# New order of work in the paired up-projection of layer 1, with its DRAM weight sums moved out of the attention

## The chip, the cores and the metric

One NeuronCore of one Trainium2 chip runs the whole network in one launch. The metric is device microseconds of one execution; a time given for a kernel is the median of its runs. In the profile PE is the matmul engine (PEld its weight loads), DVE the vector engine, ACT the scalar engine, POOL GpSimd; SP only issues DMAs, and POOL issues some too.

## The reference

A two-layer trunk on 512 tokens of width 1024 in fp32: layer 0 mixes tokens by gated linear attention (GLA), layer 1 by sparse attention with shared keys and values (NSA); each is followed by an output projection and a convolutional feed-forward. The change lies in the feed-forward of layer 1 and in what is prepared for it:

```python
def conv_ffn(x, w_up, conv_w, conv_b, w_down):
    S = x.shape[1]
    u = x @ w_up                                   # 1024 -> 2 x 2816
    u_pad = jnp.pad(u, ((0, 0), (CONV_WIDTH - 1, 0), (0, 0)))
    hc = conv_b
    for j in range(CONV_WIDTH):                    # 3 taps along the tokens
        hc = hc + conv_w[j] * u_pad[:, j:j + S]
    a, b = split_cols(hc, (FFN_DIM, FFN_DIM))
    return (jax.nn.silu(a) * b) @ w_down

h = h + conv_ffn(rmsnorm(h, norm_ffn[i]), w_up[i], conv_w[i], conv_b[i], w_down[i])
```

## The kernel before

**Precision.** Every fp32 operand of a matmul is split into a high and a low part: `split_to` lets ACT copy the high part into an fp32r tile and DVE subtract it from the source to give the low part. A product is then three matmuls (high by high, low by high, high by low). The weight tiles pass through three rings: `wraw` (four raw tiles of 128 x 1024, filled by DMAs that SP issues), and `wh` and `wl` (four split tiles each). A ring's next user waits until the last reader of the tile it takes over has finished.

**Layer 1's feed-forward.** The 2816 hidden columns are 22 blocks of 128, j = 0 to 21, each with two halves (a and b of the reference). A plain half is 24 matmuls of 128x512 into an `acc` bank of PSUM. `conv` applies the taps to a bank: one ACT instruction and two DVE instructions that write the tile `hc`. `gate` forms silu(a) * b and splits it.

From j = 6 to j = 19 the blocks go in seven pairs (`pairs`; `FAST` lists the odd members). The even block of a pair is two plain halves. The odd one is a Strassen-like scheme on 2x2 blocks: seven products of 12 matmuls of 128x256 (`product`, numbered 1 to 7; line 1131) instead of eight. Between them come the products 5, 7 and 6 of the down projection of an earlier pair (`mms`, line 1487): 5 into the banks `sc`, 7 into `po`, 6 into `pt`, six matmuls of 128x512 each. I call these the first, second and third down sum. Banks A and B of `acc` alternate, so that a bank is written again two uses later, once DVE's convolution has read it.

In a pair the names are: `w0`, `w1` the weights of the two plain halves; `w` in turn those of products 1 and 5, of 6 and 7, of 2 and 3; `wd` that of product 4; `wf` those of the first two down sums; `ops[p][6]` that of the third. `old` carries the odd block's second half into the next pair, where `second` finishes it.

**Who sets the order.** PE's matmuls here are chained by `pe`, ACT's and DVE's instructions by `Ordered` (`act.on = dve.on = True`), so each engine runs the pairs in the order in which the code is written, and an engine waits at the head of its queue. SP issues the loads in program order too, four tiles ahead (`load`).

**The sums in DRAM.** The scheme needs sums of quarters of the weight blocks. POOL prepares them in DRAM: `sums` issues four DMAs a block (a copy of 512 KB and three accumulating ones), and `pace` ties each to an instruction of the running part, so that POOL issues it then. `jobs` says which block belongs to which part: D are the 11 blocks of the down projection, U[j] the seven blocks of the up projection. Part `mix1` is the attention of layer 1, in which POOL also multiplies the probabilities P by their gates (`P<-P,ssm`).

Of the kernel before, what the change touches and what calls it, by code (L numbers as in the profile page):

```python
# [23 lines left out]
NJ = FFN // 128  # L24
# [186 lines left out]
class Trunk:  # L211
    def __init__(self, nc, tc, ctx, I, out, W):
# [21 lines left out]
        self.jobs = {"mix0": three(*D[:3]), "ffn0": each(U[7], D[3], U[9], D[4], U[11], D[5]), "mix1": three(U[13], D[6], U[15]),  # L234
                     "ffn1": each(D[7], U[17], D[8], U[19], D[9], D[10])}
# [60 lines left out]
    def early_exp(self):  # L296
        self.tc.keep_in_program_order(self.nc.scalar.activation(self.t(self.small, [128, 64], "ex", bufs=1)[:, 0:1], self.ones[:, 0:1], AF.Exp))
# [315 lines left out]
    def gla_layer(self):  # L613
        nc, I, tc = self.nc, self.I, self.tc
        with ExitStack() as outer:
            pool = outer.enter_context(tc.tile_pool(name="gla", bufs=1))
            mo = [tuple(self.t(pool, [128, S], f"mo{m}{c}", FR) for c in "hl") for m in range(2)]
# [422 lines left out]
    def up(self, l, pool, rows, us, fill, gate, pe, space=None, seven=None):  # L1040
# [44 lines left out]
        def pairs(js):  # L1085
# [6 lines left out]
            items = [(wp[up[2 * js[0]]],)]  # L1092
            for j in js:
                p, b = j // 2 - 1, self.upb(l, j + 1)
                items += [(wp[up[2 * j + 1]],), (q(qs, p, 0, 2),), (q(qd, b, 2), q(qs, b, 0)), (q(qs, b, 2), q(qs, b, 1)), (q(qs, p, 2),),
                          (q(qd, b, 3), q(qs, b, 3)), (q(qd, b, 0),), (wp[up[2 * j + 4]],)]
# [18 lines left out]
            def prep(dst=None):  # L1115
                load()
                w = dst or [self.t(self.wsp, [128, 1024], t, FR) for t in ("wh", "wl")]
                self.split_to(*w, raws.pop(0))
                return w

            def plain(half, dst, w):
                for k in range(KC):
                    o = slice(128 * k, 128 * k + 128)
                    for n, (a, b) in enumerate(((0, 0), (1, 0), (0, 1))):
                        pe(nc.tensor.matmul(dst, w[a][:, o], self.x[k][b], start=k + n == 0, stop=k == KC - 1 and n == 2))  # L1125
# [7 lines left out]
            def step(half, u, dst, *parts):  # L1133
                self.conv(l, cj[0], half, u, dst, parts)
                if "act" in parts:
                    self.pace("ffn1", self.conv_ins)

            def second(old, part):
                j, B, v, hc = old
                cj[0] = j  # L1140
                if part == 0:
                    dve.scalar_tensor_tensor(out=B[:, O], in0=v[:, E], scalar=-1.0, in1=v[:, O], op0=ALU.mult, op1=ALU.subtract)
                    dve.tensor_tensor(out=B[:, E], in0=B[:, E], in1=v[:, E], op=ALU.subtract)
                    step(1, B, hc[1], "act")
                elif part == 1:
                    step(1, B, hc[1], "dve")
                else:
                    gate(j, *hc, False)

            for _ in range(3):  # L1150
                load()
            cj, old = [0], None
            w0 = prep()
            act.on = dve.on = True
            for j in js:
                p, b = j // 2 - 1, self.upb(l, j + 1)
                hc = [self.t(pool, [128, S], "hc0", bufs=3), self.t(pool, [128, S], "hc1")]
# [11 lines left out]
                if j == js[0]:  # L1169
                    forms(2)  # L1170
                v2, = V
                v = v2.rearrange("p a t -> p (a t)")
                cj[0] = j
                step(0, A, hc[0], "act", "dve")
                ops[p] = {5: [t[:, :512] for t in wf], 7: [t[:, 512:] for t in wf]}
                mms(p, (5, 7))
                w = prep()
                step(1, B, hc[1], "act", "dve")
                act.activation(hc[0], hc[0], AF.Silu)
                A, B = (self.ps("acc") for _ in range(2))  # L1180
                product(1, A[:, E], w, 0, True)
                product(5, A[:, O], w, 512)
                w = prep()
                gate(j, *hc, False)
                act.copy(v, A)
                ops[p][6] = prep([self.t(self.tmp, [128, S], "sq", FR, bufs=2) for _ in range(2)])
                product(6, B[:, O], w, 0, True)
                product(7, B[:, E], w, 512)
                w = prep()
                wd = prep(W4[j // 2 % 2])  # L1190
                product(2, A[:, E], w, 0)
                product(3, A[:, O], w, 512)
                w0 = prep()
                dve.tensor_tensor(out=v2, in0=v2, in1=bass.AP(tensor=B.tensor, offset=B.offset + 256, ap=[B.ap[0], [-256, 2], [1, 256]]), op=ALU.subtract)
                mms(p, (6,))
                dve.tensor_tensor(out=A[:, O], in0=A[:, O], in1=v[:, E], op=ALU.add)
                hc = [self.t(pool, [128, S], "hc0", bufs=3), self.t(pool, [128, S], "hc1")]
                cj[0] = j + 1
                step(0, A, hc[0], "act", "dve")
                act.activation(hc[0], hc[0], AF.Silu)  # L1200
                product(4, B[:, E], wd, 0)
                old = j + 1, B, v, hc
            for part in range(3):
                second(old, part)
            act.on = dve.on = False
            ready.append(w0)

        for j in range(NJ):
# [15 lines left out]
            w = [ready.pop() if ready else self.wget(self.W[f"up{l}"][2 * j])]  # L1224
# [13 lines left out]
            else:  # L1238
                mm(0, range(KC))
                fill(j, 0)  # L1240
                w.append(self.wget(self.W[f"up{l}"][2 * j + 1]))
# [15 lines left out]
            self.pace(f"ffn{l}", self.conv_ins, 1 if l else 1 + j % 2 if 2 < j < NJ - 2 else 0)  # L1257
# [209 lines left out]
    def ffn_seven(self, l):  # L1467
# [206 lines left out]
        with ExitStack() as stack:  # L1674
            ap = stack.enter_context(tc.tile_pool(name=f"acts{l}", bufs=1))
            A11, A12 = ([self.t(ap, [128, T, 256], f"a{q}{c}", FR) for c in "hl"] for q in (11, 12))
# [3 lines left out]
            vec = self.t(ap, [128, 184], "taps")  # L1680
            nc.sync.dma_start(vec[:, :176], I["vec"][:, V_TAP + 176:V_TAP + 352])
            nc.sync.dma_start(vec[:, 176:], I["vec"][:, V_GAIN + 40:V_GAIN + 48])
# [88 lines left out]
    def nsa_layer(self):  # L1771
        nc, I, tc = self.nc, self.I, self.tc
        GKV, GMIX = 6, 1
        with ExitStack() as outer:
            pool = outer.enter_context(tc.tile_pool(name="nsa", bufs=1))
            K = [self.t(pool, [128, 2, S], f"K{g}", FR) for g in range(4)]
# [336 lines left out]
            with tc.tile_pool(name="nsac", bufs=2) as cp:  # L2113
# [50 lines left out]
                for s, (a, qts) in enumerate(steps):  # L2164
# [7 lines left out]
                    for i in range(6):  # L2172
# [12 lines left out]
                        if i == 3:  # L2185
                            self.pace("mix1", last[0])
# [43 lines left out]
```

## Time and profile before

| | us |
|---|---|
| median of the runs before | 1242.61 (three runs, 1239.24 to 1243.87) |
| profiled execution, its own time | 1240.31 |
| span of the profiled execution | 1238.2 |
| PE busy | 1221.2 (99%) |
| DVE busy | 940.1 (76%) |
| ACT busy | 678.6 (55%) |
| POOL busy | 185.8 (15%) |
| granted PE clock, mean | 0.999 |

Times within the execution are microseconds from its start. The attention of layer 1 lies at about 705 to 835, the feed-forward of layer 1 from about 890 to the end, the seven pairs between 951.66 and 1135. A busy PE says only that a matmul is under way: matmuls overlap, so the chain of waits, which follows from each step back to what released it, tells more than the busy share.

### The profile page before, as it was taken

What the parts mean: (1) busy time and instruction counts of PE and PEld (TensorE: products, weight loads), DVE (VectorE), ACT (ScalarE), POOL (GpSimd) and SP (SyncE); (2) the same over time, 40 slices, a digit from 0 to 9 for tenths busy, and PEclk for the clock granted to TensorE, in tenths of its full rate; (3) what the DMA queues carried; (4) which work ended last, traced back from release to release, by engine and by line L of the source; (5) the groups of instructions that cost most, each with busy time, mean ns of one, the idle gap of its engine ahead of it and who ended that gap; (6) DMA issues with size and microseconds to landing.
All of it is one profiled execution on the core that took longest, in us unless ns stands there. A gap on an engine that the chain in (4) does not pass through costs nothing.

```text
span 1238.2 us, 20022 instructions
## 1 busy us (share of the span) xinstructions
PE 1221.2 (99%) x7441; PEld 1047.4 (85%) x7441; DVE 940.1 (76%) x1722; ACT 678.6 (55%) x1299; POOL 185.8 (15%) x251
## 2 busy tenths in 40 slices
PE   9999999999999999999999999999999999998998
PEld 6888889888888888899888888888888888887886
DVE  7875887598776776878767678974799777778685
ACT  7656554455444444546535777773565445455454
POOL 1000331000000000000112166770000011000000
PEclk9999999999999999999999999999999999999999
DMA  8422841326677766344745257724456788845534
GB/s 291 122 92 76 206 86 53 118 85 196 197 173 183 186 188 170 112 144 119 216 126 182 68 151 164 174 50 126 165 153 161 186 215 218 226 132 194 167 128 153
DMA packets 65069, 190.53 MB, mean 154 GB/s; under 512 B 7679, under 2 KB 11424, under 8 KB 64428
## 3 DMA queue, kind: packets, MB, share of 16 engines
q1 hardware_dynamic: 54812, 148.99, 38.1%
q0 software_dynamic: 8352, 37.75, 15.4%
q10 hardware_dynamic: 1808, 2.51, 0.7%
q8 instruction: 59, 0.97, 0.3%
q14 instruction: 38, 0.31, 0.1%
HBM read 179.22 MB, written 41.99 MB: 179 GB/s over the span
## 4 chain that ended last, share of the span: by engine, by line
PE 91%; DVE 4%; ACT 2%; issue 1%; DMA 1%; SPq 0%; POOLq 0%; POOL 0%; ACTq 0%; DVEq 0%
PE acc L1216 25%; PE acc L1125 6%; PE acc L1012 5%; PE acc L761 4%; PE acc L372 4%; PE po L1963 3%; PE po L390 3%; PE acc L1131 3%; PE acc L1293 3%; PE po L1293 3%; PE sc L1293 3%; PE sc L1487 2%; PE po L1487 2%; PE acc L1963 2%; PE acc L390 2%; PE acc L1487 2%
## 5 line engine op out<-in xcount | busy, mean ns | idle before, releaser
L1216 PE MATMUL acc<-xh,wh 128*128 128x512 f32 x464 | 181.0, 390 | 2.8 <-DVE hc L201 1.6
L1216 PE MATMUL acc<-xh,wl 128*128 128x512 f32 x464 | 180.7, 389 | 0.0
L1216 PE MATMUL acc<-xl,wh 128*128 128x512 f32 x464 | 180.6, 389 | 0.0
L336 ACT ACTIVATE wh<-wraw 128x1024 fp32r<-128x1024 f32 x109 | 115.0, 1056 | 100.3 <-PE acc L1012 33.3
L337 DVE TENSOR_TENSOR wl<-wraw,wh 128x1024 fp32r<-128x1024 f32 x109 | 138.1, 1267 | 21.3 <-ACT wh L336 20.7
L201 DVE TENSOR_TENSOR wl<-wraw,wh 128x1024 fp32r<-128x1024 f32 (+2 forms) x95 | 108.3, 1146 | 25.8 <-ACT wh L201 22.0
L201 ACT ACTIVATE wh<-wraw 128x1024 fp32r<-128x1024 f32 (+2 forms) x95 | 93.8, 993 | 31.2 <-PE acc L1487 9.6
L1216 PEld LDWEIGHTS acc<-xh,wh 128*128 128x128 f32 x464 | 87.2, 188 | 20.8 <-ACT hc L201 2.0
L1216 PEld LDWEIGHTS acc<-xl,wh 128*128 128x128 f32 x464 | 87.1, 188 | 18.4
L1216 PEld LDWEIGHTS acc<-xh,wl 128*128 128x128 f32 x464 | 87.2, 188 | 17.3
L201 DVE SCALAR_TENSOR_TENSOR hc<-acc,h,hc 128x511 f32<-128x511 f32 x72 | 53.7, 746 | 53.2 <-ACT hc L201 52.4
L201 ACT ACTIVATE hc<-acc,h 128x512 f32<-128x512 f32 x36 | 27.9, 776 | 72.4 <-PE acc L1216 72.4
L2029 POOL TENSOR_TENSOR P<-P,ssm 128x256 f32<-128x256 f32 (+3 forms) x48 | 64.8, 1372 | 1.9
L201 DVE SCALAR_TENSOR_TENSOR hc<-acc,taps,hc 128x511 f32<-128x511 f32 x72 | 53.7, 746 | 15.0 <-ACT hc L201 13.7
L2021 ACT ACTIVATE P<-P,smn 128x128 f32<-128x128 f32 (+3 forms) x96 | 53.3, 557 | 11.0 <-DVE smn L2019 9.9
L281 POOL DMA_DIRECT2D qsum<-qsum x36 | 29.8, 851 | 195.2 <-ACT hc L201 78.1
L201 ACT ACTIVATE hc<-acc,taps 128x512 f32<-128x512 f32 x36 | 27.9, 776 | 44.2 <-DVE acc L201 23.1
L1125 PE MATMUL acc<-xh,wh 128*128 128x512 f32 x112 | 44.1, 394 | 1.2 <-DVE hc L201 1.2
L1125 PE MATMUL acc<-xl,wh 128*128 128x512 f32 x112 | 43.7, 390 | 0.0
L1125 PE MATMUL acc<-xh,wl 128*128 128x512 f32 x112 | 43.6, 390 | 0.0
L201 ACT ACTIVATE sh<-hc 128x512 fp32r<-128x512 f32 (+1 forms) x44 | 22.0, 519 | 33.5 <-DVE hc L201 29.2
L2019 DVE CUSTOM_DVE_ANT_0 P<-sc,strip 128x128 f32<-128x128 f32 (+3 forms) x72 | 29.9, 433 | 9.4 <-PE sc L1963 9.0
(646 smaller groups left out, 3588.5 us busy)
## 6 DMA issues: line engine op xcount, KB each, us to landing
wraw<-in_wp SPq DMA_DIRECT2D x174, 512.0 KB, 4.3
qsum<-in_qd POOLq DMA_DIRECT2D x18, 512.0 KB, 7.8
qsum<-qsum POOLq DMA_DIRECT2D x36, 256.0 KB, 5.6
wraw<-qsum SPq DMA_DIRECT2D x15, 512.0 KB, 4.1
wraw<-in_qd SPq DMA_DIRECT2D x15, 512.0 KB, 4.0
wraw<-qsum SPq DMA_DIRECT2D x26, 256.0 KB, 4.5
strip<-vecd SPq DMA_DIRECT2D x12, 448.0 KB, 6.0
wraw<-in_qd SPq DMA_DIRECT2D x14, 256.0 KB, 4.2
```

Source lines behind the costliest of these rows:

```text
L201: ins = f(*a, **kw)
L336: self.split_ins = nc.scalar.activation(wh, raw, AF.Copy)
L337: self.low_ins = nc.vector.tensor_tensor(out=wl, in0=raw, in1=wh.bitcast(F32), op=ALU.subtract)
L390: nc.tensor.matmul(ps[:, :N], s_, m_, start=k == 0 and n == 0, stop=k == KC - 1 and n == 2)
L1012: nc.tensor.matmul(banks[m], a[:, o], b, start=k == 6 and i == 0, stop=k == 5 and i == 2)
L1125: pe(nc.tensor.matmul(dst, w[a][:, o], self.x[k][b], start=k + n == 0, stop=k == KC - 1 and n == 2))
L1216: pe(nc.tensor.matmul(pu[half], a[:, o], self.x[k][b], start=k == 0 and n == 0, stop=k == KC - 1 and n == 2))
L1293: pe(nc.tensor.matmul(dst, a[:, o], b, start=first and n == 0 and i % 2 == 0, stop=stop and n == 2, skip_group_check=True))
L1487: pe(nc.tensor.matmul(bank[i][:, c], a[:, ts], b[:, c], start=first and n == 0, stop=stop and n == 2, skip_group_check=True))
L1963: mm = lambda *args, **kw: pe(nc.tensor.matmul(*args, **kw))
L2021: nc.scalar.activation(P[:, br, :n], P[:, br, :n], AF.Exp, scale=-1.0, bias=mn[:, br:br + 1], accum_out=f[:, j, br:br + 1])
L2029: nc.gpsimd.tensor_tensor(out=P, in0=P, in1=f[:, i, :].unsqueeze(2).to_broadcast([128, 2, 128 * t + 128]), op=ALU.mult)
```

## The change

**Order in a pair.** The third down sum moves up, to between the plain halves and product 1; the first and second move down, to between product 3 and product 4. The weights are converted a stage ahead: `split_to` is taken apart into `high` (ACT) and `low` (DVE), so that both halves can stand at different places. The weights of products 6, 7 (`wb`) and 2, 3 (`wc`) are converted while the plain halves run, `wf` and `wd` before product 1 ends, and `w0`, `w1` and `wa` (products 1 and 5) of the next pair while this one's products run. The odd block's second half is finished by `close` and `finish`, and the even block's first convolution moves ahead of the second plain half. After the last pair three converted tiles, not one, are handed on to blocks 20 and 21 (`ready`).

On ACT, around the copy of bank A (`COPY sums`) in the second pair, there stands before (`sq<-half` and `rows<-half` are the third down sum's and product 4's weights, `wh` one converted weight tile each):

```order
L201 ACTIVATE a11h_9299<-hc_1833_10188 128x256
L201 COPY sums_10025<-acc_10301 128x512
L201 ACTIVATE sq_10337<-half_10229 128x512
L201 ACTIVATE wh_10369<-wraw_10289 128x1024
L201 ACTIVATE rows_10024<-half_10327 128x512
L201 ACTIVATE wh_10404<-wraw_10339 128x1024
L201 ACTIVATE hc_1863_10416<-acc_10301,taps_9308 128x512
```

And now:

```order
L201 ACTIVATE wh_10305<-wraw_10178 128x1024
L201 ACTIVATE rows_10004<-half_10229 128x512
L201 ACTIVATE a11h_9294<-hc_1843_10199 128x256
L201 COPY sums_10005<-acc_10318 128x512
L201 ACTIVATE wh_10372<-wraw_10255 128x1024
L201 ACTIVATE wh_10379<-wraw_10262 128x1024
L201 ACTIVATE hc_1870_10421<-acc_10318,taps_9303 128x512
```

The first `wh` behind the copy was that of products 2 and 3 of the same pair; now both behind it are `w0` and `w1` of the next pair.

On PE, at the end of product 3 in the same pair, there stood the third down sum and then product 4:

```order
L1131 MATMUL acc_10301<-xl_9708,wh_10369 128x256
L1487 MATMUL pt_9580<-sq_10337,sh_10240 128x512
L1487 MATMUL pt_9580<-sq_10338,sh_10240 128x512
L1487 MATMUL pt_9580<-sq_10337,sl_10241 128x512
L1487 MATMUL pt_9581<-sq_10337,sh_10240 128x512
L1487 MATMUL pt_9581<-sq_10338,sh_10240 128x512
L1487 MATMUL pt_9581<-sq_10337,sl_10241 128x512
L1131 MATMUL acc_10302<-h_9836,rows_10024 128x256 x2
```

Now the first (`sc`) and the second (`po`, of whose six rows the first is shown) down sum stand there:

```order
L1139 MATMUL acc_10318<-xl_9703,wh_10264 128x256
L1500 MATMUL sc_9571<-wh_10305,sh_10244 128x512
L1500 MATMUL sc_9571<-wl_10306,sh_10244 128x512
L1500 MATMUL sc_9571<-wh_10305,sl_10245 128x512
L1500 MATMUL sc_9572<-wh_10305,sh_10244 128x512
L1500 MATMUL sc_9572<-wl_10306,sh_10244 128x512
L1500 MATMUL sc_9572<-wh_10305,sl_10245 128x512
L1500 MATMUL po_9573<-wh_10305,sh_10244 128x512
```

So twelve matmuls, not six, lie between the end of product 3 and product 4.

**The end of the pairs.** On ACT, behind the last pair's products, there stood before (`hc<-acc,taps` is the convolution of block 19's first half and, in the last row, of its second; `sq<-wraw` is the third quarter of down block 9, `sqacc<-wraw` a quarter of down block 10, line 336 a weight tile of block 21):

```order
L201 ACTIVATE hc_2020_11636<-acc_11528,taps_9308 128x512
L201 ACTIVATE sq_11733<-wraw_11730 128x512
L336 ACTIVATE wh_11767<-wraw_11765 128x1024
L201 ACTIVATE rows_12004<-s_1680_9304 128x512
L201 ACTIVATE rows_12025<-s_1680_9304 128x512
L201 ACTIVATE hc_2020_11636<-hc_2020_11636 128x512
L201 ACTIVATE sqacc_11839<-wraw_11833 128x512
L201 ACTIVATE hc_2021_11637<-acc_11529,taps_9308 128x512
```

And now (`wh<-more` is a weight tile of block 21, `wh<-wraw` down block 9):

```order
L201 ACTIVATE sq_11742<-wraw_11739 128x512
L201 ACTIVATE hc_2027_11647<-acc_11550,taps_9303 128x512
L201 ACTIVATE wh_11650<-more_11537 128x1024
L201 ACTIVATE wh_11744<-wraw_11738 128x1024
L201 ACTIVATE hc_2027_11647<-hc_2027_11647 128x512
L201 ACTIVATE sqacc_11842<-wraw_11836 128x512
L201 ACTIVATE rows_12007<-s_1683_9299 128x512
L201 ACTIVATE rows_12028<-s_1683_9299 128x512
L201 ACTIVATE hc_2028_11648<-acc_11551,taps_9303 128x512
```

The split of down block 9's third quarter (`sq<-wraw`) now stands ahead of the convolution of block 19's first half, on DVE too; that of down block 10 still stands ahead of the convolution of its second half.

**The sums.** The 12 jobs of part `mix1` (U[13], D[6], U[15]) leave the attention: U[13] goes to the feed-forward of layer 0, D[6] and U[15] to the one of layer 1, whose jobs become 32 instead of 24 and now reach into the last two pairs.

**Pads.** A small tile shrinks by 224 bytes a partition, which shifts what lies behind it; three pads of 224 bytes hold the tiles of the GLA, the NSA and layer 1's feed-forward where they were, and 32 bytes more in the taps tile shift those of the pool `up1` (`hc0`, `hc1`, `sh`, `sl`, `more`, `half`). The tiles of layer 0's feed-forward move by 224 bytes. No instruction is added or removed by this.

The instructions of PE, ACT and DVE are the same in number as before. The core of the diff:

```diff
-        self.jobs = {"mix0": three(*D[:3]), "ffn0": each(U[7], D[3], U[9], D[4], U[11], D[5]), "mix1": three(U[13], D[6], U[15]),
-                     "ffn1": each(D[7], U[17], D[8], U[19], D[9], D[10])}
+        self.jobs = {"mix0": three(*D[:3]), "ffn0": each(U[7], D[3], U[9], D[4], U[11], D[5], U[13]),
+                     "ffn1": each(D[6], U[15], D[7], U[17], D[8], U[19], D[9], D[10])}
...
-            for _ in range(3):
+            for _ in range(4):
                 load()
-            cj, old = [0], None
-            w0 = prep()
+            old = None
             act.on = dve.on = True
+            w0, w1, wa = (low(high()) for _ in range(3))
             for j in js:
...
                 plain(0, A, w0)
+                f2 = high(squares())
                 if old:
-                    second(old, 0)
-                w1 = prep()
-                if old:
-                    second(old, 1)
-                wf = prep()
+                    close(*old)
+                ops[p] = {6: low(f2)}
                 if old:
-                    second(old, 2)
-                plain(1, B, w1)
+                    finish(*old)
...
+                step(j, 0, A, hc[0], "act")
+                wb = high()
+                step(j, 0, A, hc[0], "dve")
+                wc = high()
+                act.activation(hc[0], hc[0], AF.Silu)
+                low(wb)
+                low(wc)
+                plain(1, B, w1)
+                mms(p, (6,))
+                step(j, 1, B, hc[1], "act")
+                wf = high()
+                wd = high(W4[j // 2 % 2])
+                step(j, 1, B, hc[1], "dve")
+                gate(j, *hc, False)
+                low(wf)
+                low(wd)
+                A, B = (self.ps("acc") for _ in range(2))
+                product(1, A[:, E], wa, 0, True)
+                product(5, A[:, O], wa, 512)
+                act.copy(v, A)
+                product(6, B[:, O], wb[0], 0, True)
+                product(7, B[:, E], wb[0], 512)
+                w0 = low(high())
+                w1 = high()
...
+                w1 = low(w1)
+                product(2, A[:, E], wc[0], 0)
+                product(3, A[:, O], wc[0], 512)
...
                 mms(p, (5, 7))
...
+                step(j + 1, 0, A, hc[0], "act")
+                wa = high()
+                step(j + 1, 0, A, hc[0], "dve")
                 act.activation(hc[0], hc[0], AF.Silu)
+                wa = low(wa)
+                product(4, B[:, E], wd[0], 0)
                 old = j + 1, B, v, hc
-            for part in range(3):
-                second(old, part)
+            close(*old)
+            finish(*old)
             act.on = dve.on = False
-            ready.append(w0)
+            ready.extend((w0, w1, wa))
...
-            self.pace(f"ffn{l}", self.conv_ins, 1 if l else 1 + j % 2 if 2 < j < NJ - 2 else 0)
+            self.pace(f"ffn{l}", self.conv_ins, (1 if l else 1 + (j % 3 > 0)) if l or 2 < j < NJ - 2 else 0)
...
-                        if i == 3:
-                            self.pace("mix1", last[0])
```

More of the change, by code (lines that the diff above doesn't have):

```diff
@@ L296, in early_exp @@
     def early_exp(self):
-        self.tc.keep_in_program_order(self.nc.scalar.activation(self.t(self.small, [128, 64], "ex", bufs=1)[:, 0:1], self.ones[:, 0:1], AF.Exp))
+        self.tc.keep_in_program_order(self.nc.scalar.activation(self.t(self.small, [128, 8], "ex", bufs=1)[:, 0:1], self.ones[:, 0:1], AF.Exp))
     def gain(self, n, k):
@@ L1113, in load, with high, low @@
                 raws.append(raw)
-            def prep(dst=None):
+            def high(dst=None):
                 load()
                 w = dst or [self.t(self.wsp, [128, 1024], t, FR) for t in ("wh", "wl")]
-                self.split_to(*w, raws.pop(0))
+                raw = raws.pop(0)
+                act.activation(w[0], raw, AF.Copy)
+                return w, raw
+            def low(part):
+                w, raw = part
+                dve.tensor_tensor(out=w[1], in0=raw, in1=w[0].bitcast(F32), op=ALU.subtract)
                 return w
@@ L1131, in product, with step @@
                         pe(nc.tensor.matmul(dst, w[a][:, o], (X if n < 4 else T)[n][k][x], start=first and k + i == 0, stop=k == 3 and i == 2, skip_group_check=True))
-            def step(half, u, dst, *parts):
-                self.conv(l, cj[0], half, u, dst, parts)
+            def step(j, half, u, dst, *parts):
+                self.conv(l, j, half, u, dst, parts)
                 if "act" in parts:
                     self.pace("ffn1", self.conv_ins)
[L1138 to L1148, printed above, removed]
@@ L1151, in pairs @@
+            squares = lambda: [self.t(self.tmp, [128, S], "sq", FR, bufs=2) for _ in range(2)]
+            for _ in range(4):
                 load()
-            cj, old = [0], None
-            w0 = prep()
+            old = None
             act.on = dve.on = True
+            w0, w1, wa = (low(high()) for _ in range(3))
             for j in js:
                 p, b = j // 2 - 1, self.upb(l, j + 1)
-                hc = [self.t(pool, [128, S], "hc0", bufs=3), self.t(pool, [128, S], "hc1")]
+                hc = columns()
@@ L1183, in pairs @@
[L1183 to L1194, printed above, removed]
@@ new lines, in pairs @@
+                product(3, A[:, O], wc[0], 512)
+                ops[p].update({5: [t[:, :512] for t in wf[0]], 7: [t[:, 512:] for t in wf[0]]})
+                mms(p, (5, 7))
+                dve.tensor_tensor(out=A[:, O], in0=A[:, O], in1=v[:, E], op=ALU.add)
+                hc = columns()
+                step(j + 1, 0, A, hc[0], "act")
+                wa = high()
+                step(j + 1, 0, A, hc[0], "dve")
+                act.activation(hc[0], hc[0], AF.Silu)
+                wa = low(wa)
@@ L1679, in ffn_seven @@
             us = self.t(ap, [128, 2 * S], "us").rearrange("p (a t) -> p a t", a=2)
-            vec = self.t(ap, [128, 184], "taps")
+            vec = self.t(ap, [128, 192], "taps")
             nc.sync.dma_start(vec[:, :176], I["vec"][:, V_TAP + 176:V_TAP + 352])
-            nc.sync.dma_start(vec[:, 176:], I["vec"][:, V_GAIN + 40:V_GAIN + 48])
+            nc.sync.dma_start(vec[:, 176:184], I["vec"][:, V_GAIN + 40:V_GAIN + 48])
             self.taps, self.norm = vec[:, :176], vec[:, 176:]
```

40 lines of the change are left out of this document (19 added, 21 removed).

## Prediction

> **What bounds the kernel now.** I read the page's first part, then PE's waits, then the chain of waits through the seven pairs. The page:
>
> ```profile
> span 1238.2 us, 20022 instructions
> PE 1221.2 (99%) x7441; PEld 1047.4 (85%) x7441; DVE 940.1 (76%) x1722; ACT 678.6 (55%) x1299; POOL 185.8 (15%) x251
> ```
>
> PE is the bound almost everywhere, so the change, which removes no matmul, can only win what PE loses by waiting: 17.0 us of idle time, and a little more where a pipeline runs empty and fills again. PE's waits over the whole execution (us in total, times, longest) say where:
>
> ```profile
> PE acc L1131 <- DVE wl L201: 3.3, 7, 0.5
> PE acc L1216 <- DVE hc L201: 1.6, 1, 1.6
> PE pt L1964 <- ACT PT L2131: 1.3, 1, 1.3
> PE acc L1125 <- DVE hc L201: 1.2, 6, 0.2
> PE acc L1216 <- ACT wh L336: 1.1, 1, 1.1
> ```
>
> Four of the five lie in the pairs or at their end: a low weight part once in each of seven pairs, a convolution once in six, and two single waits. The chain of waits (start, duration, what) shows the first block of the first pair, and one later pair from its first plain half to that of the next pair:
>
> ```profile
> 951.66 10.89 PE acc L1125 x48
> ...
> 1003.85 11.16 PE acc L1125 x48
> 1015.01 1.40 PE sc L1487 x6
> 1016.41 1.39 PE po L1487 x6
> 1017.80 2.87 PE acc L1131 x24
> ...
> 1020.69 0.03 ACT sums L201
> ...
> 1021.81 0.95 ACT wh L201
> ...
> 1022.79 1.24 DVE wl L201
> ...
> 1024.07 3.03 PE acc L1131 x23
> ...
> 1027.13 0.45 DVE acc L201
> ...
> 1027.60 0.79 ACT hc L201
> ...
> 1028.41 0.76 DVE hc L201
> ...
> 1029.19 0.76 DVE hc L201
> ...
> 1030.09 11.17 PE acc L1125 x48
> ```
>
> The chain leaves PE twice in a pair. From 1020.69 it goes through ACT's copy of bank A, the weight conversions queued behind it, and DVE's low part, whose end starts product 2's second matmul; products 6 and 7 (2.87 by the row of 24) don't cover these 3.4 us. From 1027.13 it goes through the sum on bank A and its convolution, three more instructions, to the next pair's first plain half, which writes A; six matmuls of the third down sum and product 4 don't cover these 3.0 us.
>
> **The floor of a pair.** 48 plain matmuls 10.89; three down sums 1.40, 1.39 and, for the third, 1.40 again; 84 small matmuls at 2.87 for 24, so 10.05. Sum 25.13 against 1030.09 - 1003.85 = 26.24. At the end stand PE's rows around the two single waits:
>
> ```profile
> 1134.58 0.28 PE L1131 MATMUL acc<-rows,rows 128*128 128x256 f32 x1
> 1135.99 0.47 PE L1216 MATMUL acc<-xh,wh 128*128 128x512 f32 x1 [1.14 <-ACT wh L336]
> ...
> 1141.31 0.39 PE L1216 MATMUL acc<-xl,wh 128*128 128x512 f32 x1
> 1143.34 0.47 PE L1216 MATMUL acc<-xh,wh 128*128 128x512 f32 x1 [1.64 <-DVE hc L201]
> ```
>
> From 951.66 to 1135.99 are 184.33 us; seven floors are 175.91, so 8.42 are lost up to block 20. Its first half takes 1143.34 - 1135.99 = 7.35 where 24 plain matmuls need 5.45: 1.90 more. The change has **10.3 us** to win here.
>
> **The change, part by part.** *The weights a stage ahead.* Of the conversions behind the copy, none is now for products of the same pair; `wc` stands ahead of the second plain half, over ten microseconds before product 2. That wait goes, 7 times. What is late next: `w1`. It takes the ring tile of products 6 and 7, so its high part starts when these end, then 0.95 and 1.24, 2.2 in all, ahead of the bank A sum on DVE. Products 2 and 3 last 2.87, so DVE is free 0.5 us or more before that sum can start. I cost it at nothing; the cover is these two products.
>
> *The down sums exchanged.* Between product 3 and the next pair's plain half now lie 1.40 + 1.39 + 1.43 = 4.2 us (the last is half of 2.87) instead of 2.8. The chain from 1027.13 needs 3.0, so the wait goes with 1.2 us to spare, six times and at block 20.
>
> *Do DVE and the loads keep up?* Two stretches of one pair each, the second without POOL's DMAs, by busy time:
>
> ```profile
> 1030.09:1056.34 26.25, 25.58 (x151) 22.47 (x151) 20.48 (x32) 13.15 (x20) 2.95 (x4) 1.00 0.86 213
> 1082.58:1108.81 26.23, 25.56 (x151) 22.47 (x151) 20.48 (x32) 13.15 (x20) 0.00 (x0) 1.00 0.52 155
> ```
>
> DVE's 20.48 us fit into 25.13. The DMA engines' 0.86 of 26.25 is 22.6, so a pair of 25.13 leaves a tenth free. Loads are issued when a ring tile is freed, most of a pair before use; landings of about 5 us (below) fit.
>
> *The sums in DRAM.* Pairs 6 and 7 get the four POOL DMAs that pairs 2 to 5 have. The two rows above price that: the same 26.2 us with and without. A block's DMAs on POOL, one after the other:
>
> ```profile
> 1028.68 0.52 POOL L278 DMA_DIRECT2D qsum<-in_qd  x1 [1.80 <-ACT hc L201]
> 1036.44 0.80 POOL L281 DMA_DIRECT2D qsum<-in_qd  x1 [7.24 <-DMA qsum<-in_qd]
> 1044.21 0.81 POOL L281 DMA_DIRECT2D qsum<-qsum  x1 [6.97 <-DMA qsum<-in_qd]
> 1050.34 0.83 POOL L281 DMA_DIRECT2D qsum<-qsum  x1 [5.33 <-ACT rows L201]
> ```
>
> That is 22.5 us from first to last, 2.6 less than a floor pair: no queue builds up. The last block, D[10], begins at the end of pair 6, so its first sum lands (4 to 5 us of the copy left, then 0.8 + 7) 12 to 13 us into pair 7; its load can't start before `w1`'s raw tile is free, at about 20. Cost 0. Layer 0's feed-forward takes four DMAs more; no PE wait of line 1216 but the two above exists, so its loads have slack: 0, at most some tenths.
>
> *The end of the pairs.* Now block 9's third quarter stands ahead of the bank A sum. Its load waits for `wf`'s raw tile, free some 16 us into pair 7 by my estimate (plain halves 10.9, convolution 0.79 + 2 x 0.76, product and split 1.6, low part 1.24). Landings in the busy pairs (1003 to 1083) were:
>
> ```profile
> wraw<-qsum SPq DMA_DIRECT2D x9, 256.0 KB, 5.1
> ```
>
> So it is there at 21.1; split 1.3, sum 0.45, convolution 2.3 and 0.14 of signalling give 25.3 against 25.13: 0.3 late with rounding (0 with a landing 0.3 shorter, 3 with one of 8). At block 20's second half, DVE and the split of D[10] were the cause:
>
> ```profile
> 1139.85 0.63 ACT L201 ACTIVATE sqacc<-wraw 128x512 fp32r<-128x512 f32 x1 [2.30 <-DMA wraw<-qsum]
> ```
>
> ```profile
> 1140.52 0.69 DVE L201 TENSOR_TENSOR rb<-wraw,sqacc 128x512 fp32r<-128x512 f32 x1 [2.27 <-ACT sqacc L201]
> ```
>
> Its load now starts at about 20.5 of the pair and lands at 25 to 26.5. Then DVE is the limit: from 24.8 two low parts (2.5), three splits of this size (2.1), two bank sums (0.9) and two convolution steps (1.5) end at 31.3 to 31.8, less overlap; PE wants the bank at 25.13 + 5.45 = 30.6. I keep 0.7 of the 1.90. Later waits I put at 0.3, as the loads of the last stage start nearer to their use.
>
> *Attention.* There PE waits once, 1.3 us, when these ran together:
>
> ```profile
> 779.15 4.46 POOL L2029 TENSOR_TENSOR P<-P,ssm 128x256 f32<-128x256 f32 x2
> ```
>
> ```profile
> 781.88 2.80 DVE L337 TENSOR_TENSOR wl<-wraw,wh 128x1024 fp32r<-128x1024 f32 x1
> ```
>
> The low part took 2.80 instead of the pairs' 1.24: it lay beside POOL's multiplications, which were long too, and not beside a DMA issue; both remain in the new kernel. Bounds: -1.3 if shifted times part them, +1.3 for each collision more; I take 0, since the rows of POOL there follow DVE. The Trainium skill ("SBUF — State Buffer", "Who interferes with whom") says the same: a VectorE instruction with two SBUF inputs contends with a GpSimd instruction that reads SBUF, and issuing a DMA is not of that kind. The trace agrees here (2.80 us beside 4.46). The same section speaks against the change too: VectorE in a two-port mode keeps GpSimd from writing descriptors, which would delay the sums in the pairs. By the two stretches above VectorE's 20.48 us are the same with four issues as with none, so it would change nothing in the sum; at most it makes the case of late sums likelier.
>
> *Pads.* The pools of layer 0 and 1 hold their `hc` at other places, and the same convolution takes:
>
> ```profile
> L201 DVE SCALAR_TENSOR_TENSOR hc<-acc,h,hc 128x511 f32<-128x511 f32 x72 | 53.7, 746 | 53.2 <-ACT hc L201 52.4
> L201 DVE SCALAR_TENSOR_TENSOR hc<-acc,taps,hc 128x511 f32<-128x511 f32 x72 | 53.7, 746 | 15.0 <-ACT hc L201 13.7
> ```
>
> 746 ns in both: places cost nothing.
>
> **Sum.** 10.3 - 0.3 - 0.7 - 0.3 = 9.0 us less. The profiled execution took 1240.31, so 1231.3; it lies 2.3 below the median of the runs, 1242.61, from which the sum gives 1233.6. I forecast 1232.5.
>
> **Rivals.** *Late w1 (10%).* If `w1`'s low part ends after the bank A sum could start, the convolution moves back; 0.5 + 1.2 us are free, and each further microsecond costs seven. With 0.6 us a pair the time is 1237; from 1.5 us a pair (3.2 late) the gain is gone. For it speaks that ring tiles are few; against it the 2.87 us of cover.
>
> *Late sums (8%).* If a block's four DMAs take over 25.1 us, D[9] and D[10] come late and block 20 waits. Margin for D[10] 7 us; a typical miss costs 4 to 5: 1237. For it: DMA engines at 0.86.
>
> *Stalls stay (9%).* A wait that I don't see, in DVE's order within a pair, replaces those removed: 1240. DVE has only 25.13 - 20.48 = 4.65 us to spare.
>
> *New collisions in the attention (5%), slower.* Without 12 DMA issues of 0.5 to 0.8 us POOL's multiplications can start earlier and meet DVE's low parts. Each meeting like the one above costs 1.3; seven eat the gain, twelve give 1232.5 + 15.6 = 1248. Against it: POOL mostly waits for DVE there.
>
> **How the numbers follow.** Packed pairs 68%, 1228 to 1235 by themselves: 10.3 and 1.3 from 1240.31 give 1228.7 and a fast run half a microsecond less. The first three rivals reach to 1240; I put the upper end at 1239, with one in ten above. About 0.5% (6.2 us) is what a measurement tells from no change. Faster by more, below 1236.4: 66% of the main case and half of late w1, 0.71. Slower by more: the collisions and a bad w1, 0.06. The rest, 0.23, is within.
>
> **What would show it.** Right: pairs 25.1 to 25.2 us apart, no PE wait on line 1139's low part, block 20's first half within half a microsecond of product 4, POOL's DMAs up to the end of pair 7 and none in the attention. Wrong: a new PE wait once a pair, the split of block 9 or 10 waiting for its load by more than 3 us, or more idle PE time between 705 and 835.

## The result, and the profile after

The changed kernel takes 1228.05 us (median of 4 runs, 1227.19 to 1230.37), the kernel before 1240.92 beside it (four runs): a ratio of 0.9897 with a 95% interval of 0.9869 to 0.9924, so 12.9 us less. A second set of five runs of the change, below, gave 0.9908, 11.5 us less. The forecast was 1232.5, with a range of 1228 to 1239; 1228.05 lies just inside its lower end. The profiled executions are 1227.19 and 1240.31.

The page of the changed kernel, first part, and PE's waits (us in total, times, longest):

```profile
span 1225.4 us, 20015 instructions
PE 1214.3 (99%) x7441; PEld 1044.2 (85%) x7441; DVE 943.2 (77%) x1722; ACT 680.1 (55%) x1299; POOL 183.2 (15%) x251
```

```profile
PE acc L1229 <- DVE hc L201: 1.8, 2, 1.2
PE pt L1979 <- ACT PT L2146: 1.3, 1, 1.3
```

Two things are to be seen. The waits of the pairs (line 1139 for a low part, line 1133 for a convolution) are gone, and the attention's 1.3 us stayed to the tenth. And PE's *busy* time fell, from 1221.2 to 1214.3 us, with the same 7441 matmuls. Less refilling after waits (48 plain matmuls take 10.91 us in the second pair, 11.16 in the later pair that the prediction shows) gives only a part of that. The chain through the first pair (start, duration, what):

```profile
949.46 10.88 PE acc L1133 x48
960.34 1.36 PE pt L1500 x6
961.70 8.55 PE acc L1139 x72
970.25 1.39 PE sc L1500 x6
971.64 1.36 PE po L1500 x6
973.00 1.41 PE acc L1139 x12
974.41 10.91 PE acc L1133 x48
...
1099.31 10.91 PE acc L1133 x48
```

It never leaves PE now. This first pair takes 24.95 us; the last row is the start of the seventh, which makes 24.98 on the mean of six, where the later pair in the prediction took 26.24. The forecast floor was 25.13. A part of the difference is in the down sums: six matmuls take 1.36 us where they took 1.40. The same is to be seen in layer 0, where no order was changed. The last down sums of its feed-forward, in the chain of before and then of after:

```profile
572.25 15.84 PE acc L1293 x132
```

```profile
570.75 15.40 PE acc L1306 x132
```

With these rows and those of the prediction the gain can be laid out by stages. Up to the end of layer 0's feed-forward (588.09 and 586.15) 1.94 us are won, from there to the first pair (951.66 and 949.46) 0.26, from the first pair to block 20's second half (1143.34 and 1130.62) 10.52, and 0.08 in the rest. The sum is 12.8, the difference of the spans.

At the end of the pairs, PE's rows of the changed kernel:

```profile
1124.01 0.28 PE L1139 MATMUL acc<-rows,rows 128*128 128x256 f32 x1
1124.32 0.47 PE L1229 MATMUL acc<-xh,wh 128*128 128x512 f32 x1
...
1129.62 0.39 PE L1229 MATMUL acc<-xl,wh 128*128 128x512 f32 x1
1130.62 0.47 PE L1229 MATMUL acc<-xh,wh 128*128 128x512 f32 x1 [0.61 <-DVE hc L201]
```

Block 20's first half starts 0.31 us after the last product's matmul (0.12 is the usual step), its second half 1.00 after the last of the first (usual 0.23): 0.2 us is left of the wait ahead of the first half (1.41 from start to start before), and 0.8 of the 1.90 that the first half took too long.

### The profile page after: what moved, and what is told of

It is laid out like the page before. It is cut to its first block, busy times and chain, and to the rows that moved or that the text cites. A ratio compares the mean times of both kernels' runs of the same rounds, so it can differ in the third digit from the quotient of the medians.

```text
span 1225.4 us, 20015 instructions
## 1 busy us (share of the span) xinstructions
PE 1214.3 (99%) x7441; PEld 1044.2 (85%) x7441; DVE 943.2 (77%) x1722; ACT 680.1 (55%) x1299; POOL 183.2 (15%) x251
## 4 chain that ended last, share of the span: by engine, by line
PE 89%; DVE 6%; DMA 2%; issue 2%; ACT 1%; SPq 0%; POOLq 0%; POOL 0%; DVEq 0%; ACTq 0%
PE acc L1229 21%; PE acc L1133 6%; PE acc L1013 5%; PE acc L1139 5%; PE acc L762 4%; PE acc L372 3%; PE po L1978 3%; PE po L390 3%; PE acc L1306 3%; PE sc L1500 2%; PE po L1500 2%; PE acc L1978 2%; PE po L1306 2%; PE sc L1306 2%; PE acc L390 2%; PE acc L1500 2%
## 5 line engine op out<-in xcount | busy, mean ns | idle before, releaser
L337 DVE TENSOR_TENSOR wl<-wraw,wh 128x1024 fp32r<-128x1024 f32 x107 | 135.6, 1267 | 18.1 <-ACT wh L336 17.6
L281 POOL DMA_DIRECT2D qsum<-in_qd x18 | 15.0, 846 | 144.2 <-ACT hc L201 88.4
```

Of the source, the lines that this page charges most:

```text
L337: self.low_ins = nc.vector.tensor_tensor(out=wl, in0=raw, in1=wh.bitcast(F32), op=ALU.subtract)
```

## The experiments

Each ratio is to runs of the kernel before on the same chip, with a 95% interval.

| kernel | median us | ratio | interval |
|---|---|---|---|
| the change | 1228.05 | 0.9897 | 0.9869 to 0.9924 |
| pads_alone | 1236.53 | 0.9967 | 0.9955 to 0.9979 |
| without_pads | 1231.44 | 0.9925 | 0.9911 to 0.9940 |
| sums_alone | 1241.10 | 1.0006 | 0.9995 to 1.0017 |
| order_alone | 1228.93 | 0.9914 | 0.9899 to 0.9928 |
| cover_halved | 1231.70 | 0.9931 | 0.9915 to 0.9948 |
| third_weights_late | 1229.42 | 0.9917 | 0.9900 to 0.9933 |
| shift_32 | 1228.94 | 0.9913 | 0.9893 to 0.9932 |
| best_of_parts | 1225.84 | 0.9883 | 0.9868 to 0.9897 |
| hold_alone | 1226.25 | 0.9891 | 0.9878 to 0.9905 |
| the change again | 1228.55 | 0.9908 | 0.9893 to 0.9924 |
| shift_16 | 1230.82 (one run) | | |
| pace_mended | 1226.05 | 0.9880 | 0.9864 to 0.9897 |

### The parts, one by one

**The pads alone.**

```diff
-        ... self.t(self.small, [128, 64], "ex", bufs=1) ...
+        ... self.t(self.small, [128, 8], "ex", bufs=1) ...
+            self.t(pool, [128, 56], "pad")        # in gla, acts1, nsa
-            vec = self.t(ap, [128, 184], "taps")
+            vec = self.t(ap, [128, 192], "taps")
```

> The kernel before with the pads alone (the small tile of 8 instead of 64 columns, the three unused tiles, the taps tile of 192). Theory: part of the gain comes from the places of the tiles: matmuls of the down sums run at 116.7 ns instead of 120 ns for 256 columns (layer 0) and at 227 instead of 233 ns for 512 columns (layer 1), which is worth 2.7 and 1.4 us: 1236.8 against 1240.9, and the stalls of the pairs stay. Rival: places cost nothing, as the prediction had it, and the shorter spacing comes from the new order or from the moved sums: 1240.9 and 120 and 233 ns.

Measured: 0.9967, so 4.1 us less (2.6 to 5.6). PE's waits of the pairs are those of before; in the chain, layer 0's last down sums and one of layer 1's:

```profile
PE acc L1132 <- DVE wl L201: 3.3, 7, 0.5
...
PE acc L1126 <- DVE hc L201: 1.2, 6, 0.2
```

```profile
569.29 15.40 PE acc L1294 x132
...
960.66 1.36 PE sc L1488 x6
```

Both rates came with the pads, and the stalls stayed. 15.40 us for 132 matmuls is 116.7 ns each against 120; layer 0's down sums are 924 matmuls, so 3.1 us. In layer 1 the six take 227 ns each against 233; 198 such matmuls make 1.3. Together 4.4, and the times of the runs say 4.1. The theory holds.

**The order and the sums, at the old places.** The whole change without the lines above.

> The changed kernel with its tiles at the old places: new order and moved sums, no pads. Theory: the down sums go back to 120 and 233 ns, 4.1 us are lost again: 1232.2, pairs 25.1 us apart. Rival (the order or the sums shorten the spacing): 1228, pairs 24.98 us apart.

```profile
952.93 10.89 PE acc L1132 x48
963.81 1.40 PE pt L1499 x6
...
977.99 10.91 PE acc L1132 x48
```

1.40 us are back, a pair takes 25.06 us, and the ratio of 0.9925 is 9.3 us: without the pads the change brings what the prediction's sum said, 9.0.

**The moved sums alone.**

```diff
-  "ffn0": each(U[7], D[3], U[9], D[4], U[11], D[5]), "mix1": three(U[13], D[6], U[15]),
-  "ffn1": each(D[7], U[17], ...
+  "ffn0": each(U[7], D[3], U[9], D[4], U[11], D[5], U[13]),
+  "ffn1": each(D[6], U[15], D[7], U[17], ...
-            self.pace(f"ffn{l}", self.conv_ins, 1 if l else 1 + j % 2 if 2 < j < NJ - 2 else 0)
+            self.pace(f"ffn{l}", self.conv_ins, (1 if l else 1 + (j % 3 > 0)) if l or 2 < j < NJ - 2 else 0)
-                        if i == 3:
-                            self.pace("mix1", last[0])
```

> The kernel before with the sums in DRAM moved out of the attention and nothing else. Theory: the attention does not get shorter (PE's wait of 1.3 us stays) and the one new wait of 1.2 us near 311 us comes with the moved sums: 1242.1 against 1240.9. Rival 1: the attention gains where POOL's twelve DMA issues go, 1.3 us or more: 1239.6 or less. Rival 2: the wait near 311 us is not from the sums; no change, 1240.9.

Measured: 1.0006, 0.7 us more with an interval from 0.6 less to 2.1 more. The times don't decide; the waits do:

```profile
PE acc L1216 <- DVE hc L201: 3.3, 3, 1.2
PE pt L1964 <- ACT PT L2131: 1.3, 1, 1.3
```

The attention's wait is unchanged, so rival 1 falls. Of the three waits of line 1216 one of 1.2 us is new, near 311 us. What made it: POOL's second sum, before the change and in this kernel, and the load that lies beside it there, a piece of the chain of waits:

```profile
292.26 0.84 POOL L281 DMA_DIRECT2D qsum<-in_qd  x1 [5.47 <-DMA qsum<-in_qd]
```

```profile
297.12 0.84 POOL L281 DMA_DIRECT2D qsum<-in_qd  x1 [10.68 <-ACT hc L201]
```

```profile
297.64 9.88 DMA wraw<-in_wp
```

In the first block that gives sums, the new rhythm gives one where the old gave two. So the second sum waits for a later convolution and starts 4.9 us later, beside a load of weights that takes 9.88 us (the slowest there took 7.7 before). A wait of 0.4 to 1.5 us stands there in all nine profiles taken with this rhythm, and in none of the five without it.

**The order alone.** Only `pairs` and the lines that hand on `w0`, `w1`, `wa`.

> The kernel before with the new order of the pairs alone; sums and places as before. Theory: the order takes 9.7 us by removing PE's two waits of each pair and most of the two at their end: 1231.2; pairs 25.1 us apart, no wait for a low part. It may take another 0.6 at the second half of block 20, if that wait of the changed kernel comes from the later sums. Rival: the order alone brings what all three bring together, 1228; or, if it needs the sums to be out of the way, less than 5 us: above 1236.

Measured: 0.9914, 10.7 us less (8.9 to 12.5): what was expected with the 0.6 at block 20, 10.3. The times alone don't settle it against the rival, that the order brings all that the change brings, since the second set of runs of the change gave 11.5; the rows do: the pads' gain and the moved sums' wait stand in the runs of each alone. No wait of the pairs is left, and at block 20 both halves follow one another:

```profile
1104.77 10.91 PE acc L1132 x48
...
1129.85 10.91 PE acc L1228 x48
```

From 1104.77 to 1129.85 are 25.08 us, and the 48 plain matmuls of both halves run without a gap. The kernel below with the order and the pads but without the moved sums shows no PE wait at block 20 either. So the 0.2 and 0.8 us that the changed kernel keeps there come with the moved sums, not with the order. The split of block 9's third quarter in the two kernels, the order alone first and then the change:

```profile
1123.97 0.63 ACT L201 ACTIVATE sq<-wraw 128x512 fp32r<-128x512 f32 x1
```

```profile
1120.09 0.63 ACT L201 ACTIVATE sq<-wraw 128x512 fp32r<-128x512 f32 x1 [1.69 <-DMA wraw<-qsum]
```

ACT takes it 19.2 us after the pair's start (1104.77) and waits for nothing; with the moved sums it takes it 20.8 after (from 1099.31 on), having waited 1.69 us for the load. SP issues that load 16.1 us after the pair's start in both (at 1120.90 and 1115.44); with the moved sums it lands after 4.6 us, without them after at most 3.1.

### What in the order does it

**Half the cover.**

```diff
+                ops[p].update(...)
+                mms(p, (7,))
                 product(2, A[:, E], wc[0], 0)
                 product(3, A[:, O], wc[0], 512)
-                ops[p].update(...)
-                mms(p, (5, 7))
+                mms(p, (5,))
```

> The changed kernel with one of the two down sums that stand between product 3 and product 4 put ahead of product 2, so that the sum and the convolution of bank A lie beside 1.36 + 1.41 = 2.8 us of matmuls, as before the change, instead of 4.1. Theory: that wait alone comes back, about 0.2 us and 0.3 us of running empty in each pair and at block 20: pairs 25.4 to 25.5 us apart, 1231 to 1232 against 1228; no wait for a low part. Rival: the weights a stage ahead freed DVE early enough, and the exchange of the down sums was not needed: 24.98 us, 1228.

```profile
PE acc L1133 <- DVE hc L201: 1.2, 6, 0.2
```

```profile
974.72 11.16 PE acc L1133 x48
...
1000.17 11.16 PE acc L1133 x48
```

The very wait of before, 1.2 us in six times, is back, and the pairs are 25.45 apart: 0.47 more a pair, 1231.70 us. That wait went because two down sums lie there and not one.

**The third weights late.**

```diff
-                wc = high()        # ahead of the second plain half
-                low(wc)
                 act.copy(v, A)
+                wc = high()
+                low(wc)
```

(with its load moved to its new turn)

> The changed kernel with the weights of products 2 and 3 loaded and split where they were split before the change, behind the copy of bank A, instead of ahead of the second plain half. Theory: PE waits for their low part again, 0.5 us and 0.15 of running empty in each pair; the split also pushes the next weights back, whose cover of 0.5 + 1.2 us should hold: pairs 25.6 to 25.7 us apart, 1232.5 to 1233.5 against 1228. Rival (the case of late w1 in the prediction): the cover does not hold, the convolution of bank A moves back too: pairs 26.2 us or more, 1237 or more.

```profile
974.40 10.91 PE acc L1133 x48
...
999.60 10.91 PE acc L1133 x48
```

```profile
PEld acc L1139 <- DVE wl L201: 1.1, 7, 0.2
```

25.20 us: only 0.2 more a pair, 1229.42, a third of what was expected. The wait for the low part is back in each of the seven pairs, at the weight load of product 2's second matmul, but it is 0.16 us and not 0.5. Before the change, the split of the third down sum's weights stood between bank A's copy and these weights; in this kernel it does not. ACT's row of that split before the change, then ACT and DVE here:

```profile
1021.17 0.64 ACT L201 ACTIVATE sq<-half 128x512 fp32r<-128x512 f32 x1
```

```profile
989.55 0.59 ACT L201 COPY sums<-acc 128x512 f32<-128x512 f32 x1 [0.68 <-PE acc L1139]
990.04 2.01 ACT L201 ACTIVATE wh<-wraw 128x1024 fp32r<-128x1024 f32 x2
...
991.14 2.36 DVE L201 TENSOR_TENSOR wl<-wraw,wh 128x1024 fp32r<-128x1024 f32 x2
```

From the start of the copy to the end of the low part it took 3.34 us before (1020.69 to 1024.03, rows in the prediction); here it takes 2.8 (989.55 to 992.3, the end of the first of the two low parts in the last row), about the 2.87 of products 6 and 7, which begin 0.2 us ahead of the copy. So the wait of before had two parts: the weights stood behind the copy, and the third down sum's split (0.64 us) stood ahead of them. That the 0.4 us a pair that did not come back are the split's is read from the rows and was not tried by itself. The case of a late `w1` did not come up.

### Places

The tiles' start addresses in the built kernels: x, weights, h, rows start 32 bytes past a multiple of 64. The down sums' own tiles started 32 past one in layer 0 and at one in layer 1; the pads turned both about.

**Everything moved by 32 bytes.**

```diff
+        self.t(self.const, [128, 8], "front")
-            vec = self.t(ap, [128, 192], "taps")
+            vec = self.t(ap, [128, 184], "taps")
```

> The changed kernel with a tile of 32 bytes ahead of all others and the taps tile of 184 columns again: what PE reads as x, h, rows and weights now starts at a multiple of 64 bytes (32 past one before), the down sums' tiles of layer 0 at 32 past one, as before the change, those of layer 1 at 32 past one, as after it. Theory 1: the place of the moving operand counts. 256-column matmuls then take 116.7 instead of 120 ns in the pairs (588 of them, 2.0 us less), 120 again in layer 0's down sums (2.7 more), and 512-column ones get faster too, 223 instead of 226.7 ns (about 1900 plain ones, 6.5 us less): about 1222. Theory 2: for 512 columns it is the stationary operand that counts, and one at a multiple of 64 bytes is the slow one, as in layer 1 before the change: 233 instead of 226.7 ns for the plain ones, 13 us more: about 1242. Rival: only the distance between the two operands counts: plain matmuls stay at 226.7 and the pairs' products at 120 ns, layer 1's down sums go to 233: about 1232.

```profile
569.77 15.40 PE acc L1307 x132
...
984.59 1.40 PE pt L1501 x6
986.00 8.55 PE acc L1140 x72
...
998.77 10.91 PE acc L1134 x48
```

Theories 1 and 2 fall: plain matmuls (10.91 for 48) and the pairs' products (8.55 for 72), where both operands moved, are unchanged to 0.01 us, although all of them now start at a multiple of 64. Layer 1's down sums, where only the moving operand moved, are back at 1.40. Layer 0's kept 15.40: both of its operands changed sides. The rival's rule fits these rows; its time of 1232 was worked out wrong, since by the rule layer 0 loses nothing, and 1228.94 fits. The down sums and the plain matmuls go by whether the two operands start at the same place of 64 bytes (first the moving operand's place, then that of the stationary one, which is loaded into PE ahead):

| columns | same place | different places |
|---|---|---|
| 256 (layer 0's down sums) | 120 ns (32 and 32) | 116.7 (0 and 32; 32 and 0) |
| 512 | 226.7 (32 and 32; 0 and 0) | 233 (32 and 0; 0 and 32) |

For 256 columns 64 bytes is not the whole of it. In the pairs' products every operand starts 32 past a multiple of 64, before the change and after it, and yet two steps are seen. The changed kernel's rows, twelve matmuls apart:

```profile
965.80 0.28 PE L1139 MATMUL acc<-h,wh 128*128 128x256 f32 x1
...
967.21 0.28 PE L1139 MATMUL acc<-xh,wh 128*128 128x256 f32 x1
...
968.65 0.28 PE L1139 MATMUL acc<-xh,wh 128*128 128x256 f32 x1
```

The first twelve, two in three of which have `h` as the moving operand, take 1.41 us, the next twelve, on `x`, 1.44. By the matmuls' starts the step behind one on `h` is 117.0 ns (224 of them), behind one on `xh` or `xl` 119.6 (245). In the built kernel `h` starts 32 and the weights 96 past a multiple of 128 bytes, `x` and the weights both 96. So in these products places 64 bytes apart count as different.

**Sixteen bytes.** The down sums' tiles get 772 columns, of which the first four are left out.

> The changed kernel with the first 16 bytes of each of the down sums' tiles left unused, so that in layer 0 the moving operand starts 16 or 48 past a multiple of 64 bytes, by turns, and in layer 1's pairs the stationary high part 48 and the low part 16 past one, while the weights start 32 past one. In layer 0's tail the tiles start 0 and 32 past one by turns. Theory 1, halves: what counts is whether both operands start in the same half of 64 bytes. Layer 0: 116.7 ns at 16, 120 at 48, and in the tail 116.7 at 0 and 120 at 32; layer 1: 226.7 for the high part, 233 for the low part. Theory 2, equal places only: 116.7 at 16 and at 48, 233 for both parts. About 1229 in either case.

```profile
323.50 1.42 PE pt L1306 x12
...
349.57 1.40 PE pt L1306 x12
```

```profile
998.72 1.40 PE sc L1500 x6
```

In layer 1 six matmuls, four with the stationary part 48 past a multiple and two with it 16 past, take 1.40 us, six times 233 ns; by "halves" the four would run at 226.7 and the six take 1.37, so "halves" falls there. In layer 0's steps twelve take 1.40 to 1.42, by turns, against 1.40 and 1.44 by "halves": nearly the fast rate for both. Equal places only fits these two better. The tail goes by neither: by either rule the sums' tiles that start 32 past a multiple should step by 120 ns and those at one by 116.7, but by the matmuls' starts they step by 117.7 and 117.8 on the mean. So a full rule for 256 columns stays open, and why the sign turns between 256 and 512 columns stays open too.

### One wait added, without the moved sums and with them

In the profiles of the pads alone and of the order alone PE waits 1.8 and 1.9 us near 650 us, for DVE's instruction that fills `hid`, a small tile of layer 1's attention; in those of before and after it does not. The next three kernels follow that up. In the first two of the three, one wait is added, in `project`:

```diff
+                if a == 1:   # POOL's multiplication of the weights waits for DVE's hid
+                    tc.add_manual_dep(self.pool_ins.ins, self.hid_ins.ins.name, ... Sync ...)
```

**Order, pads and this wait, sums where they were.**

> The new order and the pads with the sums in DRAM where they were before the change, and one wait added: the second of POOL's multiplications of the attention's query weights, 1.9 us, waits for DVE's instruction of 0.28 us that fills hid. In the two kernels whose profiles show PE waiting 1.8 us there, POOL had started first and DVE's instruction took 2.0 us. Theory: without the moved sums the wait at 311 us and that in block 20 go, 1.8 us, and no execution is some 3 us longer than the others: 1225.4 against 1228, spread under 1.5 us. Rival: neither the sums nor this meeting of POOL and DVE moves the time: 1228, with some runs at 1230.

**The change, and this wait.**

> The changed kernel, its moved sums and all, with only the wait of POOL's multiplication for DVE's filling of hid. Theory: the executions that are 2 to 3 us longer than the others go, the shortest stay: median 1227.3, spread under 2 us; what is left against the best version, 1225.8, is the cost of the moved sums, 1.5 to 1.8 us. Rival: the longer executions have another cause: median 1228, spread 3 us as in the changed kernel.

**The change again.**

> The changed kernel once more, for a comparison on one chip: 1228.05, with a spread of 3 us, some executions with PE's wait for hid.

The change again ran from 1226.17 to 1230.94, and its profile caught a case; its wait, the tile's row (the last number of the three is the longest, in ns), and POOL:

```profile
PE pt L1902 <- DVE hid L1951: 2.0, 1, 2.0
```

```profile
L1951 DVE SCALAR_TENSOR_TENSOR hid<-cth,chu x2: 282/1139/1996, 632.1 to 647.5; 128x124 f32<-128x124 f32 x2
```

```profile
647.48 1.90 POOL L333 TENSOR_TENSOR wraw<-wraw,h 128x1024 f32<-128x1024 f32 x1 [2.69 <-PE acc L372]
```

DVE's 0.28 us became 2.00, because it started a few hundredths after POOL's 1.90 us. With the wait it comes first:

```profile
L1951 DVE SCALAR_TENSOR_TENSOR hid<-cth,chu x1: 286/286/286, 646.8 to 646.8; 128x124 f32<-128x124 f32 x1
```

```profile
646.96 1.91 POOL L333 TENSOR_TENSOR wraw<-wraw,h 128x1024 f32<-128x1024 f32 x1 [2.86 <-PE acc L372]
```

The runs then lie between 1225.65 and 1227.50, a spread of 1.9 us against 4.8, and the median is 2.3 us lower than that of the change on the same chip, and 1.05 lower than expected. PE's wait went, and the spread fell as the theory said; that each longer execution had this wait is not shown, since one execution of a kernel is profiled. The best of the parts takes 1225.84 (1224.73 to 1226.74, a spread of 2.0 where under 1.5 was expected): 14.5 us less than before, and by the medians 2 to 3 less than the change. Its profile has neither the wait near 311 us nor one at block 20. The two intervals of the version with moved sums (0.9878 to 0.9905) and without (0.9868 to 0.9897) overlap, so that the moved sums' cost, 1.2 and 0.8 us by the changed kernel's rows, is not resolved by the times: the 1.5 to 1.8 us that were expected between the two versions came out as 0.4.

**The rhythm mended.**

```diff
-  (1 if l else 1 + (j % 3 > 0))
+  (1 if l else 1 + (j % 3 < 2))
```

> The kernel with the added wait of POOL for hid and all the moved sums, but layer 0's feed-forward gives two sums to its first step that gives any, as before the change, and one to every third step after (j % 3 < 2 instead of j % 3 > 0). Theory: the wait at 311 us came from one sum of 512 KB started 4.6 us later, beside the next loads of weights, and not from the four more that this stage takes: POOL's second sum starts near 292 us again, no load takes 9.7 us there, no wait at 311 us, 1225.0 against 1226.3. Rival: the four more sums make the loads late wherever they stand: the wait stays there or comes back later in the stage, 1226.3 or more.

```profile
293.30 0.84 POOL L281 DMA_DIRECT2D qsum<-in_qd  x1 [5.11 <-DMA qsum<-in_qd]
```

The second sum is back near 292 (this execution runs 1.9 us late from the start), no load there takes over 7.9 us, and PE's wait at 311 us is gone: in the profile it was the rhythm, not the four sums more. The time, 1226.05, is not to be told from 1226.25.

## Why the prediction was right, and where it was not

- *The pairs' stalls, 10.3 us to win with block 20.* Right. The order alone brings 10.7 (8.9 to 12.5). Both waits went, each by what was named, as the halved cover and the late weights show, but the third down sum's split had a share in the first that I did not name.
- *The floor of 25.13.* Slightly high: 25.06 at the old places, since the 72 small matmuls in a row take 8.55 us, not three times 2.87, those on `h` being the faster ones; the pads take it on to 24.98, just below the 25.1 to 25.2 that the prediction named as a sign.
- *The late `w1`, DVE's load, a lack of DMA engines.* None came up.
- *A block's four sums within 25.1 us.* Too short: in the change's profile the last two blocks take 28.1 and 27.5 us from the first issue to the end of the last, against the 22.5 read before, and in that of the change with the added wait 24.2 and 23.9. The 4 to 5 us of the rival did not follow: PE's wait at block 20's second half is 0.6 us in the first of the two profiles and 1.2 in the second.
- *Block 20: 0.3 and 0.7 kept.* Measured 0.2 and 0.8. The sizes are right, the cause only in part: I laid them to the order (the raw tile of `wf`, DVE's queue), and the order alone keeps neither. They come with the moved sums: block 9's load is issued at the same time in the pair and takes longer to land.
- *Layer 0's four sums more: "0, at most some tenths".* Too low: 1.2 us of wait. The argument, that no PE wait of line 1216 exists there and loads therefore have slack, overlooked that the expression of the rhythm also moved the *first* block's second sum.
- *Attention: 0.* Right. The wait of 1.3 us is the same in all kernels.
- *Pads: "places cost nothing".* This step failed, and it is the largest miss, 4.1 us. The row that I read was a convolution on DVE, 746 ns at either place. That says nothing of PE, which reads the same tiles as operands; rows for PE were at hand, 1.40 us for a down sum's six matmuls in layer 1 against 10.89 / 8 = 1.36 for six plain ones.

The terms that were short, 4.1 for the pads and 1.2 for the sums' wait, nearly add up to the miss: 9.0 + 4.1 - 1.2 = 11.9, between the 12.9 and the 11.5 of the two sets of runs. Of the rest the floor explains half a microsecond, and the times don't resolve more.

That the time still fell into the range, by 0.05 us, was luck. Its lower end stood for full pairs and 1.3 us won in the attention, which did not come; what carried the time there were the pads, put at nothing. The mechanism of the pairs was right: without the pads the change takes 9.3 us less than before (7.4 to 11.0), where the sum said 9.0.

## What to carry to other kernels

When matmuls of one shape run at two rates in a profile, the places of their operands are a suspect before the schedule is, and a pad of 32 bytes tests it. A wait of a few tenths that recurs in every round is closed by moving work whose operands are ready into the gap; halving the cover by one piece shows whether that was it. A rhythm rule for background transfers is read at its first turn, not only by its total.

## What the runs showed of the hardware

- The step between matmuls depends on where the two operands start relative to one another: 32 bytes apart in 64 against the same place, 116.7 against 120 ns for 256 columns and 233 against 226.7 for 512, with opposite signs; and in the pairs' products 64 bytes apart in 128 gives 117.0. The Trainium skill ("SBUF — State Buffer", "Who interferes with whom") lists PE's two read ports, for the moving operand and for loading weights, as independent. That alone would not lead one to expect that their places matter; the measurement decides.
- A DVE instruction of 0.28 us that starts just behind a POOL instruction of 1.90 us (0.04 us behind it in the change's second profile) takes 2.00. The same section of the Trainium skill says that a VectorE instruction with two SBUF inputs contends with a GpSimd instruction that reads SBUF. The trace agrees: where DVE starts 0.1 us ahead, as in the change's first profile, it keeps its 0.29 us. So 0.14 us in the start settles 2 us of PE's time.
